# Staging tiles, the place of four weight casts, and the K groups of a down projection in an encoder step

## The chip, the cores and the metric

The kernel runs on one core of one Trainium2 chip. The metric is the device time of one execution in microseconds (us), as the median of several runs. Lower is better.

## The reference

The kernel computes one step of a one-layer streaming encoder, for a prompt of 1024 rows and 64 rows of a running stream, together 1088 columns of 1024 channels. All data is fp32.

```python
xn  = rmsnorm(x);  z, xbc, dt, q, k, v, g_ssm, g_att = split(xn @ w_in)
y   = group_rmsnorm((ssd_scan(silu(conv4(xbc)), dt) + d * xs) * silu(z))      # (T, 2048)
o   = rmsnorm(differential_attention(q, k, v))                                # (T, 1024)
mix = sigmoid(g_ssm) * (y @ w_branch_ssm) + sigmoid(g_att) * (o @ w_branch_attn)
x   = x + mix @ w_out
ha, hb = split(rmsnorm(x) @ w_up)                                             # 2 x (T, 2816)
x   = x + (silu(conv3(ha)) * hb) @ w_down
```

The outputs are x, the new keys and values, and the states of the scan and of both convolutions.

## The kernel before

Rows of channels lie on the 128 partitions, and time runs along the free axis, in three stretches of 384, 384 and 320 columns (`WIDE`, index x = 0, 1, 2) or in quarters of 272 (`QW`). Every fp32 product is made of three matmuls: each operand is split into a rounded part (`hi`, a cast) and a rest (`lo`, a subtraction), and `product` (L144 to L150) adds hi by hi, lo by hi and hi by lo. A block of weights is loaded, cast on ScalarE and subtracted on VectorE (`weights`, L140 to L142). The order on each engine is set by a scheduler that simulates a timeline while it reads the program; `tc.high_priority` moves instructions ahead in it, and `tc.issue_after(i)` keeps the instructions of its block behind i on that instruction's engine. Instructions of one engine run in that order.

Three places of the program matter here.

**The product y @ w_branch_ssm.** The 2048 rows of y are taken in two halves. The scan leaves y in DRAM, span by span (`y_sc`, stored at L754), from SBUF tiles of the tags "in" (128 x 6 x 384, two buffers) and "zin" (128 x 4 x 384, two buffers) for its inputs. The first half runs beside the scan's end, the second behind it. `branch` (L184 to L211) goes by turns of two blocks of weights m, and in a turn by x: for each (x, m) it takes the neighbours (g_sc, n_sc, m_sc, loaded at L180), makes a product of 24 matmuls, and evacuates its bank: on ScalarE (L197) in the first half, on VectorE (L201, L203, L204) in the second. The operand of a half is made by `branch_rows` (L160 to L174): eight rows are loaded into staging tiles (L171), cast (L172) and subtracted (L173). `stage()` and `side()`, which give the staging tiles, the neighbours and the results, draw on one ring of tiles, tag "b_r", with 11 buffers. For the second half `last_rows(x)` (L807 to L812) does this on GpSimd (POOL), each time the first half is done with the x of its last product (m = 7). The second half's results go through `mixed` (L832 to L840: cast on ScalarE, subtraction on VectorE) into the operand of w_out.

**The plain pairs.** The up projection is made in 22 pairs of 128 hidden rows (ha and hb). The first two are plain products (`pair_plain`, L1107 to L1149, copies L1127 to L1129), the other 20 use seven products where eight blocks are multiplied (`PARTS`, after Strassen and Winograd), each in two halves s, so a pair has 14 piles of matmuls (L1062). The left operands are sums of weight blocks, made by `left_parts` (L950 to L980): POOL adds (L960, L961, L971, L978), ScalarE casts (L865), VectorE subtracts (L866). `left[2]`, those of the first such pair, are written out behind the plain pairs' first piles; the norm ahead (`norm`, its last step L225) still runs beside them.

**The down projection.** The 22 blocks of hidden rows are the K of w_down. They are taken in three groups of `DOWN` = (8, 8, 6) blocks (L33); a group has four items j, each again of 14 piles (`pair_down`, L1170 to L1222), and a pile has (blocks / 2) x 3 matmuls of 128x272. The first two groups add their results into DRAM with an accumulating DMA (L1219), the last adds x and stores. During the last item before a group, `hidden_part` (L1040 to L1050) loads the group's hidden rows (`hr`, L1048), casts them on ScalarE (L1049) and subtracts them on VectorE (L1050), two blocks at a time (128x544) and a single one (128x272) where the half of a group is odd. The part for pile p is made behind pile p of that item. Evacuations of the piles are on ScalarE (L1198, L1206) and VectorE (L1200, L1208, L1212, L1214, L1216).

Of the kernel before, what the change touches and what calls it, by code (L numbers as in the profile page):

```python
# [9 lines left out]
F32 = mybir.dt.float32  # L10
# [7 lines left out]
P = 128  # L18
D = 1024
# [10 lines left out]
FT = DFF // P  # L30
NORM = (128, 256, 192, 192, 192, 128)
LN_EXP = "natural_log_exp_and_others"
DOWN = (8, 8, 6)  # L33
QW = T // 4
ROWS = dict(fa=8, fb=8, fu=4, fs=2, fp=3, fh=2)
PARTS = ("b11", "t2", "b21", "t3", "t1", "t4", "b22")
# [39 lines left out]
def hybrid_layer(ctx: ExitStack, tc: tile.TileContext, xT, prm, cst, rope, wvd, win, wbs, wba, wout, wup, wdn,  # L76
                 ckT, cv, st0, yT, kT, v, ssm, conv, ffn):
    nc = tc.nc
    V, S, G, PE = nc.vector, nc.scalar, nc.gpsimd, nc.tensor
# [13 lines left out]
    o_sc, y_sc = scratch("o_sc", [2 * D, T]), scratch("y_sc", [2 * D, T])  # L93
# [67 lines left out]
    def branch_rows(stage, src, x, copy=S.copy):  # L161

        c, w = WIDE[x]
        hi, lo = (xn_pool.tile([P, KT, w], R32, name=f"b_{u}{x}", tag=f"{u}{x}") for u in ("hi", "lo"))
        for k in range(8):
            if stage is None:
                for u, t in enumerate((hi, lo)):
                    load(out=t[:, k].bitcast(F32), in_=src[D * u + P * k : D * u + P * (k + 1), c : c + w])
            else:
                t = stage()[:, :w]  # L170
                load(out=t, in_=src[P * k : P * (k + 1), c : c + w])  # L171
                copy(hi[:, k], t)  # L172
                V.tensor_tensor(out=lo[:, k], in0=t, in1=hi[:, k], op=ALU.subtract)  # L173
        return hi, lo  # L174
# [490 lines left out]
    with (tc.tile_pool(name="sin", bufs=1) as sin, tc.tile_pool(name="sp", bufs=1) as sp,  # L665
# [140 lines left out]

        def last_rows(x):  # L807
            assert scanned
            parts.append(branch_rows(stage, y_sc[D:], x, G.tensor_copy))
            if x == 0:  # L810
                for m in TURNS[0]:
                    loaded[m, 0] = neighbours(side, 0, (n_sc, m_sc), m, *WIDE[0])  # L812
# [293 lines left out]

    def pair_plain(f, w):  # L1107

        pre, hb, u1, u2, put, end_first, end_second, to_second = pair_rows(f)
        banks = {}  # L1110

        def pile(r, h, name, s, start, stop):
            if start:
                banks[r, s] = acc(QW)
            ps = banks[r, s]
            b = B[name, s]
            for k in range(4):
                c = slice(P * (4 * h + k), P * (4 * h + k + 1))
                for t, (x, y) in enumerate(((0, 0), (0, 1), (1, 0))):
                    PE.matmul(ps, w[r][x][:, c], b[y][:, k], start=start and k == t == 0, stop=stop and k == 3 and t == 2,  # L1120
                              skip_group_check=name == "b21")
            return ps

        yield
        for s in range(2):
            for r, u in enumerate((u1, u2)):
                S.copy(u[:, s], pile(r, 0, "b11", s, True, True))  # L1127
            S.copy(pre[0][:, 2 + QW * s : 2 + QW * (s + 1)], pile(0, 1, "b21", s, False, True))
            S.copy(hb[0][:, QW * s : QW * (s + 1)], pile(1, 1, "b21", s, False, True))  # L1129
        put(0, end_first())  # L1130
        yield
        for s in range(2):
            for r in range(2):
                pile(r, 0, "t1", s, True, False)
                ps = pile(r, 1, "b22", s, False, True)
                if r == 0:
                    to_second(ps, u1, s)
                else:
                    V.tensor_tensor(out=hb[1][:, QW * s : QW * (s + 1)], in0=ps, in1=u2[:, s], op=ALU.add)
        end_second()  # L1140
        yield
# [90 lines left out]
    def more_left(i):  # L1232
        x = next(coming, None)
        if x is not None:
            left.setdefault(i, []).append(x)

    pairs = [pair_plain(f, plain[f]) for f in range(2)]
    for u in pairs:
        next(u)
# [1 line left out]
        next(u)  # L1241
    for s in range(2):
        last_differences(s)
    left[2] = list(left_of(2, "fa"))
    for u in pairs:
        next(u)
    for i, (g, f) in enumerate(work[2:], 2):
# [123 lines left out]
```

## Time and profile before

| | us |
|---|---|
| median of 3 runs | 2482.29 (2481.93 to 2483.47) |
| the profiled execution | 2477.45 |
| its span, first to last instruction | 2475.7 |
| mean granted TensorE clock | 0.995 |
| ScalarE (ACT) busy | 1139.1 |
| VectorE (DVE) busy | 1596.5 |
| GpSimd (POOL) busy | 705.2 |

The span is what the instructions of the profiled execution cover; 1.75 us of it lie around them. The profile gives each instruction's start and length, what ended the idle time ahead of it, and the TensorE clock that was granted, as a share of full speed. Lines of the trace name tiles by the program's names: `mm` and `mx` are PSUM banks, `b_f` a staged row, `b_g` a neighbour or a result, `hr` hidden rows, `down` a result of the down projection. Matmuls overlap, so their single lengths say less than the distance of their starts.

### The profile page before, as it was taken

What the parts mean: (1) busy time and instruction counts of PE and PEld (TensorE: products, weight loads), DVE (VectorE), ACT (ScalarE), POOL (GpSimd) and SP (SyncE); (2) the same over time, 40 slices, a digit from 0 to 9 for tenths busy, and PEclk for the clock granted to TensorE, in tenths of its full rate; (3) what the DMA queues carried; (4) which work ended last, traced back from release to release, by engine and by line L of the source; (5) the groups of instructions that cost most, each with busy time, mean ns of one, the idle gap of its engine ahead of it and who ended that gap; (6) DMA issues with size and microseconds to landing.
All of it is one profiled execution on the core that took longest, in us unless ns stands there. A gap on an engine that the chain in (4) does not pass through costs nothing.

```text
span 2475.7 us, 44723 instructions
## 1 busy us (share of the span) xinstructions
PE 2433.8 (98%) x16958; PEld 2355.8 (95%) x16958; DVE 1596.5 (64%) x2735; ACT 1139.1 (46%) x2517; POOL 705.2 (28%) x736
## 2 busy tenths in 40 slices
PE   8999999999999999999999999899999999999999
PEld 7999999999999999998888989899999999999999
DVE  7326254865777667546667784665687777676765
ACT  6234343644565545438655562224443333344541
POOL 3000000000011001005334333103566676665435
PEclk9999999999999999999999999999999999999999
DMA  5217249454454354255689763656234343458875
GB/s 167 78 49 282 73 178 296 141 158 129 128 155 122 120 165 118 92 176 160 199 265 313 233 194 132 218 172 195 71 111 151 115 140 126 135 180 227 223 171 165
DMA packets 272151, 403.61 MB, mean 163 GB/s; under 512 B 32544, under 2 KB 206240, under 8 KB 271808
## 3 DMA queue, kind: packets, MB, share of 16 engines
q1 hardware_dynamic: 263872, 387.39, 48.9%
q0 software_dynamic: 4608, 8.91, 2.4%
q10 hardware_dynamic: 3456, 4.46, 0.5%
q8 instruction: 133, 2.18, 0.4%
q14 instruction: 82, 0.67, 0.1%
HBM read 267.11 MB, written 133.56 MB: 162 GB/s over the span
## 4 chain that ended last, share of the span: by engine, by line
PE 69%; DMA 4%; DVE 4%; ACT 2%; issue 2%; SPq 1%; POOL 0%; DVEq 0%; ACTq 0%; POOLq 0%
PE mx L1062 17%; PE mm L148 9%; PE mm L150 9%; PE mm L149 9%; PE mm L1062 7%; PE po L596 3%; PE mx L150 2%; PE mx L148 2%; PE mx L149 2%; PE sc L549 1%; PE sc L548 1%; PE pt L577 1%; PE mx L1120 1%; PE ye L717 1%; PE yi L711 1%
## 5 line engine op out<-in xcount | busy, mean ns | idle before, releaser
L148 PE MATMUL mm<-xn_hi,w_hi 128*128 128x384 f32 (+1 forms) x1416 | 470.5, 332 | 0.9 <-DVE zr L444 0.9
L150 PE MATMUL mm<-xn_hi,w_lo 128*128 128x384 f32 (+1 forms) x1416 | 468.5, 331 | 0.4 <-DVE w_lo L142 0.4
L149 PE MATMUL mm<-xn_lo,w_hi 128*128 128x384 f32 (+1 forms) x1416 | 467.1, 330 | 0.0
L148 PEld LDWEIGHTS mm<-xn_hi,w_hi 128*128 128x128 f32 x1416 | 266.6, 188 | 5.3 <-issue 2.0
L150 PEld LDWEIGHTS mm<-xn_hi,w_lo 128*128 128x128 f32 x1416 | 266.7, 188 | 2.9 <-issue 0.8
L149 PEld LDWEIGHTS mm<-xn_lo,w_hi 128*128 128x128 f32 x1416 | 266.6, 188 | 1.8 <-issue 0.6
L142 DVE TENSOR_TENSOR w_lo<-w_f,w_hi 128x1024 fp32r<-128x1024 f32 (+1 forms) x120 | 153.2, 1278 | 124.1 <-ACT w_hi L141 123.2
L1062 PE MATMUL mx<-n,wh 128*128 128x272 f32 x1092 | 209.3, 289 | 2.5 <-ACT u L1198 1.8
L1062 PE MATMUL mx<-m,w_hi 128*128 128x272 f32 x1050 | 201.5, 289 | 4.2 <-DVE down L1212 2.2
L141 ACT CAST w_hi<-w_f 128x1024 fp32r<-128x1024 f32 (+1 forms) x120 | 125.8, 1049 | 142.0 <-PE mm L149 86.1
L1062 PEld LDWEIGHTS mx<-n,wh 128*128 128x128 f32 x1092 | 171.6, 188 | 3.1 <-ACT u L1198 2.3
L1062 PEld LDWEIGHTS mx<-m,w_hi 128*128 128x128 f32 x1050 | 166.3, 190 | 4.9 <-DVE down L1212 2.6
L1062 PE MATMUL mx<-n,wl 128*128 128x272 f32 x546 | 157.8, 289 | 0.0
L148 PE MATMUL mm<-b_hi,w_hi 128*128 128x384 f32 (+1 forms) x448 | 147.2, 329 | 6.2 <-ACT b_g L197 6.2
L1062 PE MATMUL mx<-m,w_lo 128*128 128x272 f32 x525 | 152.1, 290 | 0.0
L150 PE MATMUL mm<-b_hi,w_lo 128*128 128x384 f32 (+1 forms) x448 | 145.9, 326 | 0.0
L149 PE MATMUL mm<-b_lo,w_hi 128*128 128x384 f32 (+1 forms) x448 | 145.8, 326 | 0.0
L461 POOL COPY pre<-pre 128x3 f32<-128x3 f32 x48 | 13.0, 271 | 454.9 <-ACT pre L462 330.7
L473 DVE SCALAR_TENSOR_TENSOR cc<-pre,par,cc 128x384 f32<-128x384 f32 (+1 forms) x216 | 126.5, 586 | 23.7 <-ACT cc L471 18.6
L562 ACT ACTIVATE p_t<-sc,mx 128x1024 f32<-128x1024 f32 (+5 forms) x144 | 106.0, 738 | 75.0 <-DVE mx L553 36.7
L700 POOL TENSOR_SCALAR_AFFINE_SELECT bc<-bc 128x1024 f32<-128x1024 f32 (+1 forms) x36 | 40.6, 1127 | 253.4 <-ACT e L687 251.1
L865 ACT CAST w_hi<-ws 128x512 fp32r<-128x512 f32 (+1 forms) x64 | 38.9, 608 | 158.6 <-PE mx L1062 112.9
(377 smaller groups left out, 6723.7 us busy)
## 6 DMA issues: line engine op xcount, KB each, us to landing
w_f<-in_win_dram SPq DMA_DIRECT2D x76, 512.0 KB, 3.7
w_f<-in_wup_dram SPq DMA_DIRECT2D x44, 512.0 KB, 3.7
hr<-q_sc SPq DMA_DIRECT2D x70, 272.0 KB, 4.6
bc<-a_sc SPq DMA_DIRECT2D x32, 512.0 KB, 6.3
q_sc<-hb SPq DMA_DIRECT2D x44, 272.0 KB, 2.3
gb<-q_sc SPq DMA_DIRECT2D x44, 272.0 KB, 3.9
x_sc<-cc SPq DMA_DIRECT2D x48, 192.0 KB, 2.2
q_sc<-gb SPq DMA_DIRECT2D x33, 272.0 KB, 2.3
```

The source lines that it names most:

```text
L141: S.copy(hi, w)
L142: V.tensor_tensor(out=lo, in0=w, in1=hi, op=ALU.subtract)
L148: PE.matmul(ps, a_hi, b_hi, start=i == 0, stop=False)
L149: PE.matmul(ps, a_hi, b_lo, start=False, stop=False)
L150: PE.matmul(ps, a_lo, b_hi, start=False, stop=i == n - 1)
L473: V.scalar_tensor_tensor(cc[:, :m], pre[:, i : i + m], cw(i), cc[:, :m], ALU.mult, ALU.add)
L548: PE.matmul(ps[:n, a : a + b], lhs, r_hi, start=True, stop=False)
L562: act(p_t[:n, :nk], sc[c][:n, :nk], AF.Exp, bias=mx[:n, c : c + 1], accum_out=dst)
L596: PE.matmul(po[:n, :P], a_t[b // 4][:kw, b % 4 * P : b % 4 * P + n], rhs, start=b == 0, stop=b == nb - 1)
L700: G.affine_select(bc[:L, :, :L], bc[:L, :, :L], [[0, 8], [1, L]], ALU.is_ge, -1e30, base=0, channel_multiplier=-1)
L865: S.copy(hi, src)
L1062: PE.matmul(ps, w[x][:, c], b[y][:, k], start=start and k == t == 0, stop=k == nk - 1 and t == 2, skip_group_check=not start)
```

## The change

1. `last_rows` no longer draws its staging tiles from the ring: for each x it takes one tile of the scan's tag "in" for six rows and one of the tag "zin" for two.
2. `left[2]` is made inside `tc.issue_after(copied.ins)`, where `copied` is the last copy of the plain pairs into `hb`. On ScalarE the four casts of that call move behind it; three of them now stand ahead of the table load for silu (L1084), one behind the first silu.
3. `DOWN` becomes (6, 8, 8). The host packs w_down by it.

```diff
-DOWN = (8, 8, 6)
+DOWN = (6, 8, 8)
...
         def last_rows(x):
             assert scanned
-            parts.append(branch_rows(stage, y_sc[D:], x, G.tensor_copy))
+            six = sin.tile([P, 6, 384], F32, name="b6", tag="in", bufs=2)
+            two = sin.tile([P, 4, 384], F32, name="b2", tag="zin", bufs=2)
+            eight = chain((six[:, k] for k in range(6)), (two[:, k] for k in range(2)))
+            parts.append(branch_rows(lambda: next(eight), y_sc[D:], x, G.tensor_copy))
...
     def pair_plain(f, w):
 
+        nonlocal copied
...
-            S.copy(hb[0][:, QW * s : QW * (s + 1)], pile(1, 1, "b21", s, False, True))
+            copied = S.copy(hb[0][:, QW * s : QW * (s + 1)], pile(1, 1, "b21", s, False, True))
...
+    copied = None
     pairs = [pair_plain(f, plain[f]) for f in range(2)]
...
-    left[2] = list(left_of(2, "fa"))
+    with tc.issue_after(copied.ins):
+        left[2] = list(left_of(2, "fa"))
```

The number of instructions on each engine stays as it was. In the changed kernel the lines stand 3 later behind L809 (L843 is the L840 of before, L869 the L866, L1053 the L1050), and 4 later in the pairs and the down projection (L1131 is L1127, L1204 is L1200, L1212 is L1208).

On SP, which issues the loads, at the end of the scan (the last stores of `y_sc`, the state at L732, weights at L140), before:

```order
L754 DMA y_sc<-y 128x4x384
L140 DMA w_f<-in_wbs_dram 128x1024 x2
L732 DMA out_dram<-state 128x512
L754 DMA y_sc<-y 128x4x384
L140 DMA w_f<-in_wbs_dram 128x1024
L732 DMA out_dram<-state 128x512
L140 DMA w_f<-in_wbs_dram 128x1024
L754 DMA y_sc<-y 128x4x320
L171 DMA b_f<-y_sc 128x384 x8
L180 DMA b_g<-g_sc 128x384
```

And now, from the first of these weights on (`b_16327` and the like are the slices of the scan's tiles):

```order
L140 DMA w_f<-in_wbs_dram 128x1024
L171 DMA b_16327<-y_sc 128x384 x6
L140 DMA w_f<-in_wbs_dram 128x1024
L171 DMA b_16328<-y_sc 128x384 x2
L732 DMA out_dram<-state 128x512
L754 DMA y_sc<-y 128x4x384
L140 DMA w_f<-in_wbs_dram 128x1024
L732 DMA out_dram<-state 128x512
L171 DMA b_16423<-y_sc 128x384 x6
L140 DMA w_f<-in_wbs_dram 128x1024
L171 DMA b_16424<-y_sc 128x384 x2
L754 DMA y_sc<-y 128x4x320
```

The rows of x = 0 moved ahead of two stores of y, those of x = 1 ahead of one; the six neighbours follow behind the last store, and behind them the rows of x = 2, in the tiles that x = 0 had.

On VectorE, at the end of the second half's first turn (evacuations L201, L203, L204 of 128x320, subtractions of `mixed`, and the weights' `w_lo` for the next turn), before:

```order
L840 TENSOR_TENSOR m_16570<-b_g,m_16569 128x224
L201 TENSOR_TENSOR b_g<-b_g,mm 128x320
L203 SCALAR_TENSOR_TENSOR b_g<-b_g 128x320
L142 TENSOR_TENSOR w_lo<-w_f,w_hi 128x1024
L204 TENSOR_TENSOR b_g<-b_g 128x320
L840 TENSOR_TENSOR m_16570<-b_g,m_16569 128x48
L201 TENSOR_TENSOR b_g<-b_g,mm 128x320
L840 TENSOR_TENSOR m_16574<-b_g,m_16573 128x272
L203 SCALAR_TENSOR_TENSOR b_g<-b_g 128x320
L142 TENSOR_TENSOR w_lo<-w_f,w_hi 128x1024
```

And now:

```order
L843 TENSOR_TENSOR m_16548<-b_g,m_16547 128x160
L843 TENSOR_TENSOR m_16552<-b_g,m_16551 128x224
L201 TENSOR_TENSOR b_g<-b_g,mm 128x320 x2
L203 SCALAR_TENSOR_TENSOR b_g<-b_g 128x320
L142 TENSOR_TENSOR w_lo<-w_f,w_hi 128x1024
L203 SCALAR_TENSOR_TENSOR b_g<-b_g 128x320
L204 TENSOR_TENSOR b_g<-b_g 128x320
L142 TENSOR_TENSOR w_lo<-w_f,w_hi 128x1024
L204 TENSOR_TENSOR b_g<-b_g 128x320
```

The first `w_lo` stood behind the evacuation of one of the turn's last two products, and now stands behind both; on TensorE four matmuls of the next product that need no `w_lo` stand ahead of the first that does.

On VectorE, at the start of the last item of the first group (hidden subtractions L1050, weights L866, evacuations L1200 and L1208), before, where this item has 8 K blocks:

```order
L1050 TENSOR_TENSOR n_25488<-hr,n_25487 128x544 x2
L866 TENSOR_TENSOR wl<-w_f,wh 128x512
L1200 TENSOR_TENSOR u_25446<-mx,u_25445 128x272
L1050 TENSOR_TENSOR n_25498<-hr,n_25497 128x544 x2
L1050 TENSOR_TENSOR n_25540<-hr,n_25539 128x544
L1200 TENSOR_TENSOR u_25446<-mm,u_25445 128x272
L1050 TENSOR_TENSOR n_25540<-hr,n_25539 128x544
L866 TENSOR_TENSOR wl<-ws_25480,wh 128x512
L1050 TENSOR_TENSOR m_25550<-hr,m_25549 128x544 x2
L1050 TENSOR_TENSOR n_25592<-hr,n_25591 128x544 x2
L866 TENSOR_TENSOR wl<-w_f,wh 128x512
L1208 TENSOR_TENSOR u_25445<-mx,u_25445 128x272
```

And now, where it has 6:

```order
L1053 TENSOR_TENSOR n_25338<-hr,n_25337 128x544 x2
L869 TENSOR_TENSOR wl<-w_f,wh 128x512
L1204 TENSOR_TENSOR u_25302<-mx,u_25301 128x272
L1053 TENSOR_TENSOR n_25348<-hr,n_25347 128x544
L1204 TENSOR_TENSOR u_25302<-mm,u_25301 128x272
L1053 TENSOR_TENSOR n_25348<-hr,n_25347 128x544
L1053 TENSOR_TENSOR n_25384<-hr,n_25383 128x544 x2
L1053 TENSOR_TENSOR m_25394<-hr,m_25393 128x544 x2
L869 TENSOR_TENSOR wl<-ws_25330,wh 128x512
L1212 TENSOR_TENSOR u_25301<-mx,u_25301 128x272
L1053 TENSOR_TENSOR n_25430<-hr,n_25429 128x544 x2
L1212 TENSOR_TENSOR u_25301<-mm,u_25301 128x272
```

The hidden subtractions keep their number and size here; fewer of them stand ahead of the second evacuation L1204 and of the first L1212. At the step from the pairs to the first group half of the 28 subtractions are 128x272 now, and one of them stands ahead of the last pair's first evacuation on VectorE (L1159, the L1155 of before), where in before that evacuation came first.

## The prediction

> **What bounds the kernel now.** I read the page first, then the waits of TensorE, then the granted clock around the longest of them. From the page:
>
> ```profile
> span 2475.7 us, 44723 instructions
> PE 2433.8 (98%) x16958; PEld 2355.8 (95%) x16958; DVE 1596.5 (64%) x2735; ACT 1139.1 (46%) x2517; POOL 705.2 (28%) x736
> ```
>
> TensorE is busy for 98% of the span, so 2475.7 - 2433.8 = 42 us are all that any better order could win, besides stretches at a halved clock. The change leaves the number of instructions on every engine as it was. So the question is which of TensorE's waits it touches. From the waits of TensorE over the whole span (engine, line, what it waited for; us in total, times, longest):
>
> ```profile
> PE mm L148 <- ACT b_g L197: 6.2, 1, 6.2
> PE mx L1120 <- ACT u L1127: 2.4, 1, 2.4
> PE mx L1062 <- DVE down L1212: 2.2, 2, 2.1
> PE mx L1062 <- DVE hb L1163: 2.0, 1, 2.0
> PE mx L1062 <- ACT u L1198: 1.8, 2, 1.6
> PE mx L1062 <- DVE u L1208: 0.6, 1, 0.6
> PE mx L1062 <- DVE u L1155: 0.5, 1, 0.5
> PE mm L1062 <- DVE down L1212: 0.4, 1, 0.4
> ```
>
> The first is at the border between the two halves of the scan's output product, the second among the plain pairs, the others around the four items that end a phase. All three places are touched by the change. Each wait can have a second price, which the windows show (us; busy time of PE, PEld, DVE, ACT, POOL; granted clock; DMA share; GB/s):
>
> ```profile
> 1555.50:1559.40 3.90, 0.00 (x0) 0.00 (x0) 2.98 (x5) 0.40 (x1) 1.32 (x3) 0.51 0.93 309
> 1559.40:1562.40 3.00, 2.93 (x9) 2.93 (x10) 1.42 (x3) 0.45 (x2) 1.79 (x3) 0.50 0.65 238
> 1774.00:1777.40 3.40, 3.26 (x14) 3.26 (x15) 3.40 (x9) 1.30 (x5) 0.00 (x0) 0.50 0.01 2
> 2224.60:2228.00 3.40, 1.64 (x14) 1.42 (x12) 3.40 (x7) 2.01 (x4) 0.00 (x0) 1.00 0.93 294
> 2251.90:2255.30 3.40, 1.35 (x11) 1.13 (x10) 3.40 (x5) 0.00 (x0) 3.40 (x4) 1.00 0.29 89
> 2255.30:2258.70 3.40, 3.40 (x16) 3.40 (x17) 2.50 (x6) 0.00 (x0) 2.39 (x3) 0.50 0.93 273
> ```
>
> After the stretch from 2251.90 in which TensorE was busy for only 1.35 of 3.40 us, the next 3.4 us ran at clock 0.50: 16 matmuls where 27 would fit, 1.7 us lost. The stretch from 2224.60 had 1.64 us of work and cost nothing. So a wait of about 2 us or more that lies within one such stretch costs 1.7 us more, a shorter one does not.
>
> [...]
>
> **First edit, the rows of the second half.** The wait itself, and what ended it, on SP, POOL, VectorE and ScalarE in order of time:
>
> ```profile
> 1537.07 0.37 SPq L754 DMA_DIRECT2D y_sc<-y  x1
> 1537.53 4.57 SPq L171 DMA_DIRECT2D b_f<-y_sc  x8
> 1543.12 4.32 POOL L172 CAST b_hi<-b_f 128x384 fp32r<-128x384 f32 x6 [0.48 <-DMA b_f<-y_sc]
> 1550.48 1.43 SPq L171 DMA_DIRECT2D b_f<-y_sc  x3
> 1556.24 11.47 SPq L171 DMA_DIRECT2D b_f<-y_sc  x11
> 1558.08 1.35 DVE L173 TENSOR_TENSOR b_lo<-b_f,b_hi 128x384 fp32r<-128x384 f32 x2 [0.92 <-POOL b_hi L172]
> 1559.00 0.42 ACT L197 COPY b_g<-mm 128x320 f32<-128x320 f32 x1 [4.81 <-DVE b_lo L173]
> 1559.47 0.69 PE L148 MATMUL mm<-b_hi,w_hi 128*128 128x384 f32 x1 [6.22 <-ACT b_g L197]
> ```
>
> Eight staged rows, six neighbours and the results of the running products share one ring of 11 slots. The copy L197 that empties the bank of the last 128x320 product needs a slot, and it waits 4.81 us for the subtraction that frees a staged row. TensorE waits for the bank. Price: 6.22 us, and from 1559.47 to 1562.40 half speed, 2.93 / 2 = 1.47 us. Together 7.7 us.
>
> With the rows in the scan's tiles nothing staged holds a slot, so L197 can run at about 1553.3, when its product ends. What is late next? The rows of x=0: POOL cast them by 1543.12 + 4.32 = 1547.4 even with the late issue, 5.8 us ahead of need. The rows of x=2 go into the slot of x=0 and into the operand tile that the last old product frees at 1553.25: 8 casts of 4.32 / 6 = 0.72 us end near 1559, and four wide products go first. I cost the staging at nothing; the cover is those products.
>
> The order shows a new wait. At the second turn of the new half (the weights of m = 2 and 3) VectorE's first w_lo now stands behind both evacuations of the first turn's last products. The rows around that place before:
>
> ```profile
> 1584.58 0.34 PE L148 MATMUL mm<-b_hi,w_hi 128*128 128x384 f32 x1
> 1584.78 0.49 DVE L201 TENSOR_TENSOR b_g<-b_g,mm 128x320 f32<-128x320 f32 x1 [0.46 <-PE mm L150]
> 1585.54 0.48 DVE L203 SCALAR_TENSOR_TENSOR b_g<-b_g 128x320 f32<-128x320 f32 x1
> 1585.94 1.22 DVE L142 TENSOR_TENSOR w_lo<-w_f,w_hi 128x1024 fp32r<-128x1024 f32 x1
> ```
>
> Let T be the end of the turn's last product (1584.58 before). L201 starts at T + 0.20, two steps of 0.4 us follow, then 1.22 us of w_lo: T + 2.25. TensorE can do four matmuls that need no w_lo (0.17 us each, 1584.58 and its successors), until T + 0.7. New wait 1.6 us, just short of a halved clock. Behind that w_lo stand the L204 and the second w_lo, which TensorE needs one product later.
>
> Sum: -7.7 + 1.6 = **-6.1 us**. Bounds: -7.7 if the scheduler's modelled order finds w_lo done early anyway, -2 if the wait grows to 4 us and halves the clock (4 + 1.7).
>
> **Second edit, the four weight casts.** They move behind the last copy of the plain pairs (L1129). Before:
>
> ```profile
> 1772.17 1.50 DVE L225 SCALAR_TENSOR_TENSOR n<-n,n 128x272 f32<-128x272 f32 x1
> 1773.70 0.39 ACT L1127 COPY u<-mx 128x272 f32<-128x272 f32 x1 [2.02 <-DVE n L225]
> 1787.29 1.28 ACT L1084 ACT_TABLE_LOAD   x1
> 1793.08 0.44 DVE L1139 TENSOR_TENSOR hb<-mx,u 128x272 f32<-128x272 f32 x1 [3.72 <-DMA q_sc<-hb]
> ```
>
> TensorE's wait of 2.38 us and its 1.7 us of half clock hang on the copy at 1773.70, and this waited for VectorE's L225, not for a cast: ScalarE was idle for 2.02 us ahead of it. (The copy's row u takes the slot of the norm's n.) The casts taken away ahead of it gave ScalarE time that it had. I take **-0.2 us**, for earlier steps of the norm. Bounds: -4.1, if VectorE's order too lets L225 run earlier. And +1.9: three casts of about 0.62 us now stand ahead of the silu table load at 1787.29, and behind it come the gate, the store of hb and the L1139 at 1793.08 that waits for that store. The free banks of TensorE cover 1.9 us there; without them it is paid.
>
> **Third edit, the groups.** The hidden parts of the next group are cast and subtracted during the last item of the old phase. From the groups of VectorE in the last phase, its timeline, the window of the item before the second group, POOL's and ScalarE's timelines:
>
> ```profile
> L1050 DVE TENSOR_TENSOR n<-hr,n 128x544 fp32r<-128x544 f32 x30 | 27.6, 947 | 5.1 <-ACT n L1049 5.1
> L1050 DVE TENSOR_TENSOR n<-hr,n 128x272 fp32r<-128x272 f32 x6 | 3.0, 508 | 0.0
> 2214.27 2.02 ACT L1049 CAST n<-hr 128x544 fp32r<-128x544 f32 x3 [2.21 <-DMA hr<-q_sc]
> 2299.40:2320.50 21.10, 20.65 (x164) 20.43 (x164) 19.54 (x28) 14.39 (x27) 8.27 (x6) 1.00 0.86 235
> 2302.02 1.36 DVE L1050 TENSOR_TENSOR n<-hr,n 128x544 fp32r<-128x544 f32 x2 [1.21 <-ACT n L1049]
> 2304.42 4.80 DVE L1050 TENSOR_TENSOR n<-hr,n 128x544 fp32r<-128x544 f32 x3
> 2305.25 1.66 POOL L961 TENSOR_TENSOR ws<-ws,w_f 128x512 f32<-128x512 f32 x1
> 2332.70 1.07 DVE L1050 TENSOR_TENSOR m<-hr,m 128x544 fp32r<-128x544 f32 x1 [0.34 <-ACT m L1049]
> ```
>
> *Pairs to the first group.* Before, this transition costs 0.5 + 2.0 + 0.6 + 2.05 us of waits (L1155, L1163, L1208, L1212) and the halved stretch from 2255.30: 6.9 us. With six K blocks half of the 28 subtractions shrink from 128x544 to 128x272, by 947 - 508 = 440 ns in the mean, and by 0.68 - 0.51 = 0.17 us where the full ones are undisturbed (1.36 us for the two from 2302.02): 14 of them free 2.4 to 6 us of VectorE, and a quarter of the loads goes. In the new order about 3 us of waits are left with these durations, none of them of 2 us, so no halved stretch: 6.9 - 3.4 is what goes: **-3.5 us**. Bounds -6.9 and +3, since a hidden subtraction now stands ahead of the last pair's first evacuation L1155, and if its hr comes as late as at 2214.27 the evacuation waits with it.
>
> *First to second group.* Before, VectorE worked without a pause worth naming from 2302.02 to 2333.8, 31.8 us, for the 28 full subtractions and what lies between. The item from 2299.40 has 14 x 12 matmuls in 21.1 us, its successor as well, so the last part (pile 7 of 7) was needed at 2299.4 + 21.1 + 6 x 3.02 = 2338.6: 4.8 us to spare. Now the item before has 14 x 9 matmuls, 15.8 us: the last part comes 0.5 us late. With the earlier parts in their order I take 1.2 us on top of the 0.45 that this place cost: **+1.2 us**. Bounds 0 and +8.7 (5.3 us, what the item is shorter by, and two halved stretches).
>
> The three subtractions from 2304.42 took 1.6 us each, beside POOL's L960, L961 and L971, against 0.68 us for the two from 2302.02. [...] The same POOL work now falls into a shorter stretch; that speaks for the upper half of these bounds.
>
> *Second to third group.* Before 1.6 us (the long one of L1198), from a group of 8 to one of 6; now from 8 to 8 with the order of before's first such step, which cost 0.45, and with the final group's additions: **-0.6 us**, between -1.1 and +1.
>
> **Sum.** -6.1 - 0.2 - 3.5 + 1.2 - 0.6 = -9.2 us. The profiled execution took 2477.45 us (span 2475.7 and 1.75 around it), so 2468.25 by it. The median of the runs is 2482.29, 4.84 above the profiled one, for reasons the trace doesn't show; carried over: **2473.1 us**.
>
> **Rivals.**
> - *E, the plain pairs' wait goes too* (-4.1 for -0.2): 2469.2. For it: one cast stood before the norm's first steps on ScalarE. Against: the 2.02 us of idle time ahead of the copy. Chance 0.12.
> - *D, VectorE catches up at the first group* and has time to spare at the second: -6.9 for -3.5, nothing for +1.2, -1.1 for -0.6: 2482.3 - 6.1 - 0.2 - 6.9 - 1.1 = 2468. For it: the half-size subtractions free up to 6 us where 5.2 us are waited. Against: a hidden subtraction now ahead of the first evacuation. Chance 0.08.
> - *B, the first wait is only handed on*: the edit frees the ring, but w_lo becomes late by 4 to 5 us and halves the clock, so that of 7.7 us about 1 remains: 2482.3 - 1.2 - 0.2 - 2.9 = 2478. For it: the scheduler put eight mixed subtractions and two evacuations ahead of that w_lo. Against: the subtractions should be done by then. Chance 0.17.
> - *C, slower: VectorE is the bound at every step between groups*, since hidden subtractions now stand ahead of evacuations that free TensorE's banks: +3 at the pairs, +8.7 at the second group, +1 at the third, against -6.3 of the other edits: +6.4, 2488.7. It decides once the three places together cost 6.3 us more than their present 6.9 + 0.45 + 1.6 = 8.9, and shows as slower from 11.3 more. For it: the 31.8 us without a pause, and 21.1 us that become 15.8. Against: the half-size subtractions at the first place. Chance 0.15.
>
> **How the numbers follow.** The forecast has 0.48, with its own range 2470 to 2477. What a measurement can tell here from no change is about 0.2%, 5 us: 2477.3 to 2487.3. Faster: 0.43 of the forecast, all of E and D, 0.07 of B: 0.70. Same: 0.05 of the forecast, 0.10 of B, 0.03 of C: 0.18. Slower: 0.12 of C. The range from 2465.5 to 2483 holds forecast, E, D and B, and leaves C out, some 0.15 with the tails.
>
> **What would show it.** In the profile of the changed kernel: no wait for L197 near 1553 and no halved clock behind it; a wait of some 1.6 us for w_lo (L142) at the second turn of the new half, near 1577; the wait for L1127 (now L1131) still above 2 us with its halved stretch; at the first group fewer than 4 us of waits and full clock; at the second about 1.7 us. Waits of TensorE for VectorE's evacuations L1159 to L1220 above 10 us in sum would say C; a w_lo wait above 3 us, B.

## The result, and the profile after

The changed kernel takes 2475.69 us (median of 19 runs, 2472.26 to 2481.1) beside 2480.68 us for the kernel before (19 runs, 2475.2 to 2485.31). The ratio is 0.9983, with a 95% interval of 0.9975 to 0.9991: 4.2 us faster, between 2.2 and 6.2. The forecast was 9.2 us, so a little under half of it came, and 0.17% is inside the 0.2% that the prediction called no change, though the interval leaves zero out.

From the page of the changed kernel:

```profile
span 2470.6 us, 44709 instructions
PE 2431.1 (98%) x16958; PEld 2351.9 (95%) x16958; DVE 1588.6 (64%) x2735; ACT 1137.6 (46%) x2517; POOL 704.5 (29%) x736
```

TensorE's waits over the whole span:

```profile
PE mx L1065 <- DVE down L1220: 3.4, 1, 3.4
...
PE mx L1065 <- ACT u L1157: 1.4, 2, 0.8
PE mx L1124 <- ACT u L1131: 1.4, 1, 1.4
PE mx L1065 <- DVE down L1216: 1.3, 2, 0.9
PE mx L1065 <- DVE u L1159: 1.2, 2, 0.9
PE mx L1065 <- DVE u L1204: 1.2, 2, 0.8
PE mm L1065 <- DVE down L1216: 1.2, 1, 1.2
```

The 6.2 us for L197 are gone and the 2.4 us for L1127 are 1.4 us for L1131. In their place the longest wait of the matmuls between 100 us and the end is a new one, 3.4 us for L1220, the last result of the first item of the down projection.

TensorE runs the same 16958 matmuls in both kernels, so the start of the n-th matmul is a landmark. Time between landmarks in each profiled execution, in us, worked out from the traces (10000 to 10400 holds the first edit's place, 10400 to 14800 the second's, 14800 to 16800 the groups; matmuls change places inside the stretches):

```
kernel                      10000-10400  10400-14800  14800-16800   ratio to before
before                           73.66       564.55       262.48
changed                          67.54       564.02       267.95    0.9983
changed, again                   67.53       564.02       265.64    0.9981 [0.9971, 0.9992]
change without the groups        67.54       564.51       263.82    0.9975 [0.9964, 0.9986]
groups alone                     74.41       563.64       266.91    1.0011 [1.0001, 1.0021]
staging alone                    67.53       565.08       263.66    0.9966 [0.9953, 0.9979]
casts alone                      75.31       564.15       262.49    0.9995 [0.9984, 1.0006]
other tile for result 5          67.55       563.93       272.54    0.9998 [0.9988, 1.0008]
late sums                        67.56       563.90       264.66    0.9982 [0.9973, 0.9990]
other tile and late sums         67.56       563.92       269.42    0.9997 [0.9988, 1.0006]
same, weights first              67.54       564.96       267.13    0.9969 [0.9960, 0.9978]
no subtraction in group 2        67.53       564.52       263.47    0.9978 [0.9969, 0.9988]
groups (8, 6, 8)                 67.56       563.95       269.82    0.9998 [0.9988, 1.0007]
no groups, late sums             67.54       564.32       267.29    0.9978 [0.9968, 0.9987]
```

The first column tells the first edit apart within 0.05 us wherever it is in. The third tells groups (8, 8, 6) (262.5 to 263.8) from groups (6, 8, 8) (265.6 to 268.0), each without a further edit: like with like, the third edit took back 1.8 to 4.4 us of the 6.1. Each row is one profiled execution, and a half-clock stretch that falls into a column is part of it; the ratio in the last column is from the runs.

**The first edit's place.** The windows of the changed kernel show full clock and a busy TensorE where it stood before, and the timeline shows what came in 20 us later:

```profile
1555.50:1559.40 3.90, 3.90 (x25) 3.90 (x24) 2.73 (x7) 0.00 (x0) 0.00 (x0) 1.00 0.48 145
```

```profile
1572.73 0.93 DVE L201 TENSOR_TENSOR b_g<-b_g,mm 128x320 f32<-128x320 f32 x2 [1.11 <-PE mm L150]
1573.58 0.48 DVE L203 SCALAR_TENSOR_TENSOR b_g<-b_g 128x320 f32<-128x320 f32 x1
1573.69 0.44 PE L148 MATMUL mm<-b_hi,w_hi 128*128 128x384 f32 x1 [0.55 <-DVE b_g L201]
1573.98 1.22 DVE L142 TENSOR_TENSOR w_lo<-w_f,w_hi 128x1024 fp32r<-128x1024 f32 x1
1575.26 0.45 PE L150 MATMUL mm<-b_hi,w_lo 128*128 128x384 f32 x1 [0.60 <-DVE w_lo L142]
```

Here is the handed-on wait of the prediction: L201, one L203, w_lo, in that order on VectorE, and TensorE waits 0.60 us for the last of them. The other 0.55 us are for L201 itself, which frees the bank that the new product needs. 1.15 us in all, at full clock.

**The second edit's place.**

```profile
1761.21 1.51 DVE L225 SCALAR_TENSOR_TENSOR n<-n,n 128x272 f32<-128x272 f32 x1
1762.76 0.39 ACT L1131 COPY u<-mx 128x272 f32<-128x272 f32 x1 [3.77 <-DVE n L225]
1763.20 1.02 PE L1124 MATMUL mx<-n,m 128*128 128x272 f32 x6 [1.36 <-ACT u L1131]
1799.18 0.52 PE L1065 MATMUL mx<-n,wh 128*128 128x272 f32 x2 [0.80 <-ACT u L1157]
1801.90 0.52 PE L1065 MATMUL mx<-n,wh 128*128 128x272 f32 x2 [0.58 <-ACT u L1157]
```

ScalarE's copy still waits for L225, for 3.77 us now. But against TensorE's last matmul ahead of the wait L225 is 1.0 us earlier than before. From L224 to L225 VectorE works without a pause in both kernels, 16.7 us. L224 waits for the norm's step L223 on ScalarE, and it is this step that came 1.0 us earlier. In the kernel before, a weights' cast of 0.62 us (1753.98) stood ahead of the norm's steps on ScalarE, and its subtraction stood ahead of the evacuation (L888) whose square ScalarE took next:

```profile
1754.63 0.69 DVE L866 TENSOR_TENSOR w_lo<-w_f,w_hi 128x512 fp32r<-128x512 f32 x1 [3.29 <-ACT w_hi L865]
```

Both went behind the copies. Behind the wait of 1.36 us the granted clock was 1.00 (1762.40 to 1765.80, and no halved stretch up to 2244.5). 0.80 and 0.58 us come up at the next pair.

**The groups.** Timelines of VectorE, POOL, SP and TensorE in the first item of the first group, then the windows behind it:

```profile
2229.08 1.17 DVE L1086 SCALAR_TENSOR_TENSOR cc<-pre,par,cc 128x546 f32<-128x546 f32 x1
2233.14 0.77 DVE L1086 SCALAR_TENSOR_TENSOR cc<-pre,par,cc 128x546 f32<-128x546 f32 x1
2236.21 2.11 POOL L1092 TENSOR_TENSOR hb<-hb,cc 128x480 f32<-128x480 f32 x2
2238.35 0.36 SPq L1093 DMA_DIRECT2D q_sc<-hb  x1
2243.51 0.79 DVE L1218 TENSOR_TENSOR down<-mm,u 128x272 f32<-128x272 f32 x2 [5.36 <-DMA q_sc<-hb]
2245.17 0.82 PE L1065 MATMUL mx<-m,wh 128*128 128x272 f32 x2 [3.41 <-DVE down L1220]
```

```profile
2244.50:2247.90 3.40, 2.73 (x12) 2.73 (x13) 2.46 (x7) 0.00 (x0) 2.38 (x3) 0.50 0.97 291
2247.90:2251.30 3.40, 3.40 (x17) 3.40 (x17) 0.23 (x1) 0.39 (x1) 3.33 (x3) 0.50 1.05 297
```

The result of part 5 (L1218) takes its tile from the ring fh, which has two rows; its row still holds the last pair's second hb. That row is gated (L1086), multiplied on POOL (L1092), stored (L1093), and free when the store has landed, 5.07 us after its issue. VectorE waits 5.36 us at L1218, L1220 is queued behind it, and TensorE waits 3.41 us for L1220's bank and runs 6.1 us at half clock after it. In the kernel before, the same store and the same evacuation ran like this:

```profile
2253.03 0.36 SPq L1090 DMA_DIRECT2D q_sc<-hb  x1
2255.39 0.77 DVE L1214 TENSOR_TENSOR down<-mm,u 128x272 f32<-128x272 f32 x2
```

The store landed at 2255.20, 2.17 us after its issue, and the evacuation had no wait that the trace shows. Two things differ. The item lasts 15.8 us in place of 21.1, so VectorE reaches the evacuation 0.2 us ahead of the store's issue (at 2238.15) where it came 2.4 us behind it. And this store took 5.07 us to land. When the changed kernel was profiled again, it landed in 2.46 us:

```profile
2241.03 0.79 DVE L1218 TENSOR_TENSOR down<-mm,u 128x272 f32<-128x272 f32 x2 [2.74 <-DMA q_sc<-hb]
```

There VectorE waits 2.74 us and TensorE 0.80 us for L1220. So the order makes the wait, and the landing time sets its length; why it landed late in one execution and not in the other is not shown.

The steps between the groups, TensorE's waits and the subtractions ahead of the last:

```profile
2293.87 0.52 PE L1065 MATMUL mm<-m,w_hi 128*128 128x272 f32 x2 [1.16 <-DVE down L1216]
2310.34 4.41 DVE L1053 TENSOR_TENSOR m<-hr,m 128x544 fp32r<-128x544 f32 x3
2315.15 0.52 PE L1065 MATMUL mm<-n,wh 128*128 128x272 f32 x2 [0.79 <-DVE u L1212]
2316.80 0.49 PE L1065 MATMUL mx<-m,w_hi 128*128 128x272 f32 x2 [0.87 <-DVE down L1216]
```

Three waits, 2.8 us, for evacuations on VectorE that stand behind hidden subtractions. The row of 4.41 us merges three of them, and they are not alike: the first took 3.14 us, the others 0.71 us each. While the first ran, POOL was making its weight sums L964 and L974 (2309.72 to 2312.89). Ahead of the wait of 1.16 us a subtraction took 1.72 us beside POOL's L981. In this execution none of the 51 subtractions of 128x544 that had no POOL sum beside them took more than 0.73 us. The step to the third group has one wait, 0.44 us.

### The profile page after: what moved, and what is told of

It is laid out like the page before. It is cut to its first block, busy times and chain, and to the rows that moved or that the text cites. A ratio compares the mean times of both kernels' runs of the same rounds, so it can differ in the third digit from the quotient of the medians.

```text
span 2470.6 us, 44709 instructions
## 1 busy us (share of the span) xinstructions
PE 2431.1 (98%) x16958; PEld 2351.9 (95%) x16958; DVE 1588.6 (64%) x2735; ACT 1137.6 (46%) x2517; POOL 704.5 (29%) x736
## 5 line engine op out<-in xcount | busy, mean ns | idle before, releaser
L142 DVE TENSOR_TENSOR w_lo<-w_f,w_hi 128x1024 fp32r<-128x1024 f32 (+1 forms) x120 | 153.0, 1276 | 124.6 <-ACT w_hi L141 123.2
```

The costliest lines, as they stand in the source:

```text
L142: V.tensor_tensor(out=lo, in0=w, in1=hi, op=ALU.subtract)
```

## The experiments

**Each edit by itself, and the change without its third.** In the change without the groups one line differs from the changed kernel:

```diff
-DOWN = (6, 8, 8)
+DOWN = (8, 8, 6)
```

> The change with the groups of before (8, 8, 6); staging and casts stay. Theory (the groups cost time): in the two profiles the three steps into the groups cost 6.9 + 0.45 + 1.57 = 8.9 us before and 6.45 of waits + 3.1 of halved clock + 2.8 + 0.44 = 12.8 us after, so this kernel beats the changed one by about 4 us and the kernel before by 6 to 8 us (ratio 0.9968 to 0.9976); TensorE's wait of 3.4 us for L1220 is gone and its waits behind 2200 us are those of before (5 to 7 us). Rival (the 3.4 us come from the other two edits, which shift the whole end): the wait stays, and the ratio is that of the change, 0.9983.

Ratio 0.9975 (0.9964 to 0.9986), 6.2 us below before. The wait for L1220 is gone; its four waits of over 0.9 us at the first step are 1.3, 2.0, 1.5 and 1.0 us. The theory holds by the ratio to before and by the wait for L1220. Its other waits missed: behind 2200 us they add up to 9.0 us, where 5 to 7 were expected. Against the changed kernel's 0.9983 the times alone don't tell the two apart.

The groups alone (the same line the other way in the kernel before):

> The kernel before with groups (6, 8, 8) alone. Theory (the first group's short item meets the store of the last pair's second hb): TensorE waits over 3 us for the sixth or seventh pile of the first item again, VectorE's evacuation L1218 waits about 5 us for the DMA q_sc<-hb, and the step to the second group costs 2 to 3 us; time +2 to +5 us against before (ratio 1.0008 to 1.002). Rival of the prediction (half-size subtractions pay): -2 to -3 us.

1.0011 (1.0001 to 1.0021), 2.7 us slower than before. VectorE waits 4.75 us for the DMA q_sc<-hb at this evacuation, TensorE 2.81 us for what is behind it, and 1.43 + 1.30 + 0.87 us at the step to the second group, more than the 2 to 3 expected. The wait is the groups' own.

The staging alone (`six`, `two` and `eight` in `last_rows`):

> The kernel before with the rows of the second half in the scan's tiles alone. Theory: the 6.2 us wait for L197 and its halved clock are gone, 1.0 to 1.6 us of waits for b_g and w_lo come in about 20 us later; -6 to -6.5 us (ratio 0.9974 to 0.9976). Rival (the wait is only handed on to the mixed rows or to w_out): -1 to -3 us, with new waits of over 3 us before 1650 us.

0.9966 (0.9953 to 0.9979), below the expected 0.9974 to 0.9976, which lie inside the interval. New waits 0.55 and 0.58 us, close to the 0.55 and 0.60 of the changed kernel. No wait of 3 us ahead of 1650 us: the rival falls.

The casts alone (`copied` and `tc.issue_after`):

> The kernel before with the four weight casts behind the plain pairs' copies alone. Theory (VectorE's L225 holds the copy, the casts only shift): the wait of 2.4 us for L1127 falls to 1.4 us, waits of 0.8 + 0.6 us come up ahead of the first piles of the next pair; +0.4 us in waits, and -1.7 us where the halved stretch of the wait goes: -1.3 to +0.4 us (ratio 0.9995 to 1.0002). Rival (the casts set the wait): it goes as a whole with no new wait, -4 us.

0.9995 (0.9984 to 1.0006), which can't be told from no change. Waits of 1.37, 0.78 and 0.56 us, as expected.

**Where the third edit's gain went.** In the changed kernel the fifth result of the first item gets its tile from another ring:

```diff
-                c[p] = row("fp" if p in (2, 6) else "fh", "down")[:, :HALF]
+                c[p] = row("fp" if p in (2, 6) else "fb" if (g, j, p) == (0, 0, 5) else "fh", "down")[:, :HALF]
```

> The changed kernel, where the fifth result of the first item of the first group takes its tile from the ring fb (8 rows) in place of fh (2 rows); the order on VectorE is the same. Theory (the slot): that tile had to wait for the store of the last pair's second hb; so VectorE's wait of 5.4 us at L1218 and TensorE's of 3.4 us for L1220 go, and the halved clock of 6.8 us with it: -3.4 to -6 us against the changed kernel (ratio 0.996 to 0.997 against the kernel before). Rival C of the prediction (hidden subtractions fill VectorE): TensorE still waits 2 to 3 us at that item, for another evacuation, and the time is that of the changed kernel.

0.9998 (0.9988 to 1.0008): slower than the changed kernel on the same chip by 0.17%, where 3.4 to 6 us of gain were expected. L1218 no longer waits for the store, and yet TensorE waits 4.17 us, for L1216 in the second item. In order of time:

```profile
2249.60 0.36 SPq L1035 DMA_DIRECT2D gb<-q_sc  x1
2255.89 1.36 POOL L1037 TENSOR_TENSOR gb<-gb,gb 128x544 f32<-128x544 f32 x1 [5.67 <-issue]
2263.62 0.51 ACT L868 CAST wh<-ws 128x384 fp32r<-128x384 f32 x1 [8.90 <-POOL ws L964]
2264.16 0.79 DVE L869 TENSOR_TENSOR wl<-ws,wh 128x384 fp32r<-128x384 f32 x1 [7.14 <-ACT wh L868]
2265.36 0.82 PE L1065 MATMUL mx<-m,w_hi 128*128 128x272 f32 x2 [4.17 <-DVE down L1216]
```

The last pair's hidden sums reload what its late store wrote (L1035). The reload was issued 0.01 us after that store had landed and landed at 2255.76. POOL sat idle for 5.67 us in front of L1037, which needs it, and the third item's weight sums are queued behind it; ScalarE's cast waits for those, VectorE's subtraction for the cast, and L1216 stands behind the subtraction. The same store reaches TensorE by a second way. That way alone is not worth the whole wait: the weights that the queued sums need landed at 2258.81, and POOL came to them at 2260.44. So the sums were moved to the first item of the second group:

```diff
-                if p == 3 and i < FT + 2 and i % 2 == 0:
+                if p == 3 and i < FT and i % 2 == 0:
                     hidden_sums(i // 2 - 1)
+                if p == 3 and i == FT + 4:
+                    hidden_sums(FT // 2 - 1)
```

> The changed kernel, where the last pair's hidden sums (four loads, four sums on GpSimd, four stores) are made in the first item of the second group in place of the first item of the first; nothing before the third group needs them. Theory (one late store, two ways to TensorE): the store of the last pair's second hb holds the tile of the fifth result, and by the reload of what it stored it holds GpSimd's sums L1037 to L1039, behind which the weight sums L963, L964 of the third item are queued; so the second wait (2.3 us for L1216 in the second item, 4.2 us with the other tile) goes, and the slot wait (DMA q_sc<-hb at L1218) stays: -1 to -4 us against the changed kernel (ratio 0.9965 to 0.9975). Rival (GpSimd is not what the evacuation waits for): the wait for L1216 in the second item stays above 2 us in this profile, ratio 0.998.

0.9982 (0.9973 to 0.9990), no gain over 0.9981 of the changed kernel run again. The local part came as the theory had it: VectorE still waits 3.70 us at L1218, TensorE 1.86 us behind it, and the second item has no wait above 0.3 us. The gain in time did not. Against the profile of the changed kernel run again, 4.0 us go between the matmuls 14800 and 15600, and between 15600 and 16280, the step to the second group, 2.7 us come back, with waits of 4.3 us.

With both edits:

> The changed kernel with both: the fifth result's tile from the ring fb, and the last pair's sums in the second group. Theory: both ways of the late store are cut, so neither a wait for q_sc<-hb at L1218 nor one over 1 us for L1216 in the first two items is left; the steps into the first group cost less than 4 us: -4 to -6 us against the changed kernel (ratio 0.996 to 0.997). Rival (the ring fb itself, which the hidden loads use, makes the other kernel slow): as slow as that one, ratio 0.999 to 1.000.

0.9997 (0.9988 to 1.0006): the theory of two ways falls short, and the time is the rival's. TensorE waits 2.42 us for L1216 in the first item and 2.42 us for it in the second, and now POOL's sums wait for the weights' load itself. SP's and POOL's timelines, and the time to landing of the weight loads issued between 2240 and 2260 us (below, with the weights first, between 2240 and 2252 us; the hidden loads stand at L1054 there):

```profile
2243.34 3.63 SPq L1051 DMA_DIRECT2D hr<-q_sc  x6
2247.07 0.43 SPq L959 DMA_DIRECT2D w_f<-in_wdn_dram  x1
2257.20 1.03 POOL L963 TENSOR_TENSOR ws<-w_f 128x384 f32<-128x384 f32 x1 [8.36 <-DMA w_f<-in_wdn_dram]
```

```profile
DMA to landing us min/median/max: 4.3/7.1/10.0
```

Six hidden loads of the second group, 272 KB each, went out ahead of that weight load. Held behind it:

```diff
-            load(out=w[:, : 2 * n], in_=block)
+            held.append(load(out=w[:, : 2 * n], in_=block))
...
+                if g == 1:
+                    with tc.issue_after(held[2 * FT + 1].ins):
+                        load(out=t, in_=kind(name)[:, s, i0 + j : i0 + j + n])
+                else:
+                    load(out=t, in_=kind(name)[:, s, i0 + j : i0 + j + n])
```

> The kernel with the other tile and the late sums (six blocks first), where the six hidden loads of the second group that SP issued ahead of the third item's second weight load now stand behind it; nothing else moves on SP. Theory (a third way: those 272 KB loads go ahead of the weights, whose last load then landed 10 us after its issue): the wait of 2.4 us for L1216 in the second item goes, GpSimd's L963 no longer waits 8.4 us for its weights; about -2.5 us against that kernel (ratio 0.9983 to 0.999 against before), the 2.4 us in the first item and the 5 us at the second group stay. Rival (the DMA queues are full anyway, whoever goes first): the weights land as late, wait and time as in that kernel, 0.9997.

```profile
2245.78 0.33 SPq L959 DMA_DIRECT2D w_f<-in_wdn_dram  x1
2246.16 6.86 SPq L1054 DMA_DIRECT2D hr<-q_sc  x8
2250.71 1.02 POOL L963 TENSOR_TENSOR ws<-w_f 128x384 f32<-128x384 f32 x1 [1.27 <-DMA w_f<-in_wdn_dram]
```

```profile
DMA to landing us min/median/max: 3.7/4.2/4.8
```

0.9969 (0.9960 to 0.9978). The weights land within 4.8 us though the other tile still comes from fb, so that ring is not slow in itself. No wait above 0.2 us is left in the second item, and 2.3 us go between the landmarks (269.42 to 267.13), as expected. In the first item 1.11 + 0.52 us are left of the 2.4. The ratio fell by 0.28%, about 7 us, below the expected 0.9983 to 0.999 and more than that trace shows; where the rest comes from stays open. Of the two loads of weights, the one with six hidden loads ahead of it on SP landed after 10.0 us, and with none ahead of it after 4.8.

**VectorE at the second group.** In the changed kernel the subtractions of the second group are left out (GpSimd sets those lo parts to zero, so that share of the products is missing):

```diff
-                V.tensor_tensor(out=lo[:, j : j + n], in0=t, in1=hi[:, j : j + n], op=ALU.subtract)
+                if g == 1:
+                    G.memset(lo[:, j : j + n].bitcast(F32), 0.0)
+                else:
+                    V.tensor_tensor(out=lo[:, j : j + n], in0=t, in1=hi[:, j : j + n], op=ALU.subtract)
```

> The changed kernel without the 28 hidden subtractions of the second group: their lo parts are set to zero by GpSimd instead, so this part of the products is left out. Theory (VectorE is the bound at the step from the 6 to the 8 blocks, where 28 subtractions and what lies between need 31.8 us): the waits there, 1.15 + 0.79 + 0.87 = 2.8 us, fall below 0.6 us: -2 to -3 us against the changed kernel; the 3.4 us at the first item stay. Rival (the loads of hr, which come in a shorter time, are late): the waits stay above 2 us and are named after ScalarE's casts.

All three waits at the step are gone, and 2.6 us at the first item stay: VectorE's work is what TensorE waits for at the step. Smaller waits came up one item earlier (0.99 us) and one later (1.13 us). The experiment takes away the subtractions together with what POOL's sums do to them, so it doesn't tell their number from their stretching; the 1.72 and 3.14 us above speak for a large share of the second, and no run tests it alone. 263.47 us between the landmarks, 2.2 to 4.5 less than the two profiles of the changed kernel; the ratio of 0.9978 (0.9969 to 0.9988) is too coarse to show it.

Groups (8, 6, 8), one line again:

> The changed kernel with groups (8, 6, 8). Theory: the slot wait at the first item goes (that item lasts 21.1 us again), the step 8 to 6 has half-size subtractions and costs 0 to 0.5 us, and the step 6 to 8 costs the 2.8 us that it costs in the changed kernel: steps as in the (8, 8, 6) kernel within 1 us; ratio 0.9975 to 0.9985. Rival (what costs is a short group ahead of any other, by its DMAs): as slow as the changed kernel, with waits of 3 us or more at the last step.

0.9998 (0.9988 to 1.0007). The first step is as with (8, 8, 6) and the step 8 to 6 costs one wait of 0.53 us, but the step 6 to 8 is far worse than 2.8 us:

```profile
2394.97 6.72 DVE L1053 TENSOR_TENSOR m<-hr,m 128x544 fp32r<-128x544 f32 x4 [1.51 <-ACT m L1052]
2402.19 0.79 PE L1065 MATMUL mx<-m,w_hi 128*128 128x272 f32 x2 [4.91 <-DVE down L1208]
```

Four subtractions stand ahead of the final group's first L1208, and the row merges them: one took 4.75 us, the others 0.71 to 0.73 us. During the long one POOL ran three kinds of sums one behind the other (L974, L964, L1214, from 2395.63 to 2399.83). Behind the 4.91 us of wait the matmuls start 0.23 us apart where they started 0.13 us apart ahead of it: a halved stretch. The theory fails here; the rival's wait of 3 us or more at the last step is there, but the trace names a subtraction held beside POOL's sums, and ahead of it 1.51 us for a cast that waited for its load. In the two orders tried, a short group costs ahead of a group of 8, and more ahead of the last.

The sums moved late with groups (8, 8, 6):

> Staging and casts of the change, groups (8, 8, 6) as before, and the last pair's sums in the first item of the second group. Theory: the waits of 1.5 and 1.0 us for L1216 in the first two items of the down projection, which the kernel with these groups still has, fall to under 0.5 us: 1.5 to 3 us below the kernel without the late sums (ratio 0.9965 to 0.997 against before). Rival (longer items cover GpSimd's queue already): ratio 0.9975 as without.

0.9978 (0.9968 to 0.9987): by the ratio the rival holds. Of the two waits for L1216 the one of 1.0 us went and the one of 1.5 us fell only to 1.14; a wait of 1.76 us for L1212 came up just ahead of it, and one of 2.29 us at 2335 us, in the item where the sums now are.

The changed kernel again:

> The changed kernel again, beside the three others on one chip. Both theories: ratio 0.998 (0.9975 to 0.999), with the wait of about 3 us for L1220 in place. Theory of the clock (a wait of about 2 us halves the clock or not by where it falls in stretches of 3.41 us): the waits near 1210 and 1423 us are of the same 2 to 2.5 us as before, but are halved in some profiles and not in others.

0.9981 (0.9971 to 0.9992). The expectation's wait for L1220 was 0.80 us in this execution, not 3; instead L1216 in the second item was waited for 2.32 us, behind a weights' subtraction that waited 5.28 us for its cast, and this for POOL's sums: the second way of the late store in place of the first. Here too it is not the only one, since the weights for those sums had landed just 0.24 us before POOL came to them.

## Why the prediction was right or wrong

The time lies inside the range of 2470 to 2477, and that is in part luck. The change is worth 4.2 us and not 9.2; taken off the 2482.29 that the prediction started from, this gives 2478.1, outside the range. The 2475.69 lies inside because the kernel before came out at 2480.68 over more runs. By the prediction's own 0.2% the outcome counts as no change, to which it gave 0.18, against 0.70 for faster.

**First edit: right.** Forecast -6.1 us, measured 67.54 - 73.66 = -6.1 between the landmarks. The 7.7 us of wait and clock went, and 1.15 us came in at the place named. That the sum agrees to a tenth is luck: w_lo cost 0.60 us of the forecast 1.6, another 0.55 us were for L201's bank, which had no term, and 7.7 less 1.15 would be 6.55. Rival B's wait of 4 to 5 us did not come.

**Second edit: right within what can be measured.** Forecast -0.2, bounds -4.1 and +1.9. The copy still waited for L225, as forecast, but L225 was 1.0 us earlier, since the cast and its subtraction had held up the norm's first steps (rival E's argument, which the forecast put at 0.2 us), and the wait of 1.36 us in place of 2.38 had no halved stretch behind it: -1.0 and -1.7 us, with 1.4 us new at the next pair, together -1.3. The stretch between the landmarks is only 0.5 us shorter.

**Third edit, pairs to the first group: wrong, and in sign.** The step of the prediction that failed is "in the new order about 3 us of waits are left with these durations, none of them of 2 us, so no halved stretch". It costed VectorE's shorter subtractions against TensorE's old demand, and left out that the first item itself became 5.3 us shorter while the last pair's tail did not. 6.45 us of waits and 3.07 us of halved clock replaced 6.9 us: +2.6 for -3.5 in that profile, +0.3 in the other (5.5 + 1.7). The bound of +3 was for another reason, a late hr. Half of VectorE's wait of 5.36 us hangs on the store's landing time, 5.07 us here and 2.46 us in the other profile, which the prediction did not look at. What the runs put in its place: the store of the second hb, by its tile (L1218) or by POOL's queue, and, with both ways cut, the weight loads behind hidden loads on SP.

**Third edit, first to second group: right in mechanism, too small.** Forecast +1.2 on top of 0.45, measured 1.16 + 0.79 + 0.87 = 2.8, so +2.4. VectorE's subtractions are what is waited for, shown by leaving them out. The term was mis-sized because it compared only the last part with its need; the waits fell on evacuations queued between the parts, behind subtractions stretched from 0.71 to 1.72 and 3.14 us beside POOL's sums. The prediction had seen such stretching and let it speak for the upper half of its bounds, but the 1.2 us have no term for it.

**Third edit, second to third group:** forecast -0.6, measured 0.44 us for 1.57, -1.1.

Sum of the terms as measured: -6.1 - 1.3 + 2.6 + 2.4 - 1.1 = -3.5 us, beside -4.2 (-6.2 to -2.2) by the runs. The sum leaves something out: from the 10000th matmul on, the landmarks of the same two profiles make it -6.1 - 0.5 + 5.5 = -1.2 us, and those of the changed kernel run again -3.5 us. What is left out, 1.6 us at the groups and 0.8 us at the second edit, shows in no wait of over 0.2 us, and what it is stays open. Rival C named the mechanism of the second step, at 8.7 us where it cost 2.4. Rival D, time to spare at the first group, did not come.

The best ratios of the study are the staging alone (0.9966) and the changed kernel with the tile, the sums and the weights moved (0.9969, 0.9960 to 0.9978); their intervals overlap with each other and with 0.9975 of the change without its groups, so which of the three is fastest stays open. All three beat the kernel before; against the changed kernel's 0.9975 to 0.9991 none is clear by its times alone.

## What to carry to other kernels

When a stage is made shorter, ask what the stage before it still owes: a tile that waits for a store, a reload of that store, a queue behind the reload. Taking one such wait away shows the next, so follow the late thing to its source before giving it another buffer. A ring of tiles that one use holds across a DMA while the other frees TensorE's banks with it is a place to look; but the other tile alone gained nothing here (0.9998), and only with the sums and the weight load moved too did the ratio come to 0.9969. And read a row that merges several instructions one by one before its mean is used: four subtractions of 1.68 us in the mean were three of 0.7 us and one of 4.75.

## What the runs showed of the hardware

In the two profiles a hidden subtraction of 128x544 on VectorE took at most 0.73 us when POOL made no sum beside it (49 of 70 in the kernel before, 51 of 70 in the changed one). Beside POOL's sums single ones took up to 1.82 us in the kernel before, 3.14 us in the changed one and 4.75 us with the groups (8, 6, 8), where POOL's sums followed each other without a pause.

The length of a wait alone did not tell whether the clock was halved behind it. The same wait in the scan (L711) in two executions, in windows cut in stretches of 3.41 us, counted from that execution's halved ones, first the changed kernel, then the one with the weights first:

```profile
1206.90:1210.30 3.40, 2.55 (x15) 2.23 (x13) 0.00 (x0) 2.34 (x6) 2.02 (x2) 1.00 1.00 325
1210.30:1213.70 3.40, 1.75 (x22) 1.58 (x23) 2.58 (x2) 2.75 (x6) 3.32 (x3) 1.00 0.46 148
```

```profile
1210.20:1213.60 3.40, 1.23 (x8) 0.91 (x6) 0.68 (x1) 2.91 (x5) 1.99 (x2) 1.00 0.91 305
1213.60:1217.00 3.40, 3.25 (x22) 2.92 (x23) 3.40 (x3) 1.25 (x4) 2.72 (x2) 0.50 0.56 130
```

2.50 us of wait split over two stretches cost no clock; 2.33 us that fell nearly whole into one cost 1.6 us more (half of the 3.25 us of matmuls at clock 0.50). A shorter wait had a halved stretch behind it too: 1.73 us at L692 in the kernel before, just ahead of 1186.9 us, so the prediction's "about 2 us or more" is no threshold:

```profile
1183.40:1186.90 3.50, 1.77 (x22) 1.41 (x20) 2.85 (x4) 2.32 (x5) 1.81 (x2) 1.00 0.62 163
1186.90:1190.30 3.40, 3.40 (x12) 2.45 (x11) 0.00 (x0) 3.38 (x9) 1.41 (x2) 0.50 1.00 334
```

In the clock records of the kernel before, halved stretches begin at 1186.92, 1425.86, 1555.56, 1774.02 and 2255.30 us: 70, 38, 64 and 141 times 3.413 us from one to the next. In the changed kernel they begin at 2244.48 and 2469.76 us, 66 times 3.413 us apart. TensorE was not idle throughout ahead of the halved stretches in the rows above: 1.23 us of matmuls lay in the window before the one, 1.77 us in the window before the other. The wait for w_lo (L142) in the scan, near 1424 us, differs in the same way between the kernels: 2.04 us with clock 0.50 behind it (1425.90 to 1429.30) before, 2.16 us with clock 1.00 behind it (1423.90 to 1427.30) in the changed kernel. So waits of 2.0 to 2.5 us at one place cost 1.6 us more in one execution and nothing more in another; what decides beyond these rows is not shown. The kernel before spreads over some 10 us (2475.2 to 2485.3), and in the runs beside the experiments its mean clock, 0.993 to 0.998, is on the whole lower the longer the run; how much of the spread this makes is not shown. Two profiled executions alone would not have told this change: up to the 10000th matmul, where nothing was changed, they differ by 3.8 us, most of it the halved stretches of the kernel before at 1186.9 and 1425.9 us (1.7 and 1.6 us, half of their 3.40 and 3.24 us of matmuls).
